# A hybrid mLSTM, HGRN2 and SwiGLU layer: operand sums of the gate input from the normalized rows in SBUF, in four two-row tiles, and a second norm emitted by readiness

## The chip, the cores and the metric

The kernel runs on one core of one Trainium2 chip. The metric is the device time of one launch in microseconds, as the median of several runs. A profiled execution has a time of its own; its trace names every instruction with its engine: TensorE (PE, with weight loads as PEld), VectorE (DVE), ScalarE (ACT), GpSimd (POOL) and SyncE (SP), whose queue issues nearly all DMAs.

## The reference

One layer for 1024 prompt tokens and 8 sequences of 4 new tokens (1056 columns in all), model width 1024. Cut to what matters:

```python
def _layer(x, ...):
    h = _rmsnorm(x, norm_mix)
    p = h @ w_in + b_in                       # split into mLSTM (q,k,v,o,i,f) and HGRN2 (q,f,i,g) parts
    out_a, ... = _mlstm_mixer(...)            # causal conv over 4 rows, chunked mLSTM, head norm, sigmoid gate
    out_b, ... = _hgrn_mixer(...)             # chunked HGRN2, head norm, silu gate
    x = x + concat([out_a, out_b]) @ w_out
    h2 = _rmsnorm(x, norm_ffn)                # the second norm
    x = x + (silu(h2 @ w_gate) * (h2 @ w_up)) @ w_down     # D_FF = 2816
    return x, states
y = _rmsnorm(x, norm_final)
```

The states of both mixers are returned too. All is float32.

## The kernel before, in words

Activations lie transposed: the 1024 features are 8 rows k (`KT`) of 128 partitions, the 1056 tokens are columns. Each float32 operand of a large product is split into a high and a low part of a reduced format (`HI`, `LO` for activations, `whi`, `wlo` for weights), and a product is three matmuls: HI by whi, LO by whi, HI by wlo. ACT copies the high part out, DVE or POOL subtracts to get the low part.

The stages, by the trace's time:

- 0 to 36 us: start, first norm of block 0. The tokens go in three blocks of 288, 384 and 384 (`BL`). Blocks 1 and 2 are normalized by the generator `startup(b)` while block 0's products run.
- to about 270 us: the w_in products of the mLSTM part, head by head and block by block, with the mixer's small products between them; `ck`, `qB` are a head's k and q after the convolution (L573 to L590 on DVE), `go` its output gate (L623 on ACT); L685 is the q-k product of a chunk.
- to about 550 us: the same for the HGRN2 part, and the sample sequences (`sample_b`), whose states come in by DMA (`st`, L774) for the products `so` (L842). The mixer's outputs are written into the rows of X; `mix_split` splits them into HI and LO, and `x_rows` reloads x into X for the residual.
- to about 649 us: the out-projection (w_out). `out_evac` adds the residual into X, squares the row (L1210) and adds the squares up (L1214) for the second norm, and stores X to DRAM (`d_x`), for the end of the kernel. The tokens go in four quarters q of 264 (`QN`) here. `norm2(q)` normalizes a quarter in place and splits it into HI and LO.
- to about 693 us: two "plain" feed-forward tiles (`NPLAIN`), 16 units of 24 matmuls; their evictions are a silu on ACT (L1250) and a product on DVE (L1256).
- to about 1200 us: gate and up products of the other 20 tiles in a seven-product scheme (`g_step`, P1 to P7, L1466), with operand sums T1 to T4 of the activations made by `t_prep` and `t3_prep`, and sums S1 to S4 of the weights made by `gsplit` (S on DVE L1383, whi on ACT L1394, wlo on POOL or DVE L1395). P1 and P2 take HI and LO as they are; P5 and P6 take T1 and T2. ACT copies P2's result out of PSUM (L1474).
- to the end: the down-projection (L1689) and the last norm.

X is one SBUF tile of 8 rows. `norm2` stores its normalized rows to a DRAM buffer `d_h` (L1224), and `t_prep` loads them back (`fetch`, L1310) into tiles in which it may overwrite them; X itself becomes the tile of T1 and T2.

The order of the work is written by the program itself. TensorE's units stand in a list; between its matmuls `hook()` lets generators such as `startup`, `norm2` and `t_prep` emit a step each. A generator that yields a number waits for so many hooks; one that yields `need(engine, tiles...)` waits until a running estimate of all engines' times (`estimate`) has those tiles ready. Each engine runs its instructions in the order emitted, so this fixes each queue.

```python
def x_rows(m, th):                 # called after the split of each odd row
def norm2(q):
    yield from norm_gen(("q", q), xq(q), hq(HI, q), hq(LO, q), naccs[q], V_G2, N2W[q], ...)
N2W = ((3, 3), (2, 4), (5, 4), (6, 4))     # counts of hooks before the norm's two TensorE steps
TPK0 = 6                           # plain unit before which t_prep starts
```

Of the kernel before, what the change touches and what calls it, by code (L numbers as in the profile page):

```python
# [41 lines left out]
def hybrid_step(ctx: ExitStack, tc: tile.TileContext, i, o):  # L42
# [197 lines left out]
    def emit_k(u, ks):  # L240
        t, nk = u["t"], u["nk"]
        rh, rl = u["rhs"]
        n = rh[:, 0, :].shape[1]
        if ks[0] == 0:
            u["ps"] = bank(u["tag"])
# [3 lines left out]
        for k in ks:  # L249
            c = k * u["stride"] + u["coff"]  # L250
            wh, wl = hi[:, c:c + 128], lo[:, c:c + 128]
            nc.tensor.matmul(ps[:, :n], wh, rh[:, k, :], start=(k == 0), stop=False)  # L252
            if not late:
                nc.tensor.matmul(ps[:, :n], wh, rl[:, k, :], start=False, stop=False)  # L254
            nc.tensor.matmul(ps[:, :n], wl, rh[:, k, :], start=False, stop=(k == nk - 1 and not late))  # L255
# [22 lines left out]
    X = act.tile([128, KT, T], F32, tag="X", name="X")  # L278
    x2 = [X]
# [19 lines left out]
    def load_x(b):  # L299
        for m in range(0, KT, 2):  # L300
            nc.sync.dma_start(xb(b)[:, m:m + 2], i["xT"][:, m:m + 2, OFF[b]:OFF[b] + BL[b]])
# [56 lines left out]
    def norm_gen(key, x, hv, lv, acc, vg, w=(2, 3), pb=None, lo_dve=(0, 4), step=2, rows=None, late=()):  # L358

        n = x.shape[2]  # L360
# [3 lines left out]
        def low(m):  # L364
            (nc.vector if m in lo_dve else nc.gpsimd).tensor_tensor(lv[:, m, :], x[:, m, :], hv[:, m, :].bitcast(F32),
                                                                    op=OP.subtract)
        for m in range(KT):
            nc.vector.scalar_tensor_tensor(x[:, m, :], x[:, m, :], col(vg + m), pb[:, :n], op0=OP.mult, op1=OP.mult)
            nc.scalar.activation(hv[:, m, :], x[:, m, :], AF.Copy)  # L369
            if m and m - 1 not in late:  # L370
                low(m - 1)
            if m == KT - 1:
                for j in (*late, m):
                    low(j)
            if rows and m % 2:
                rows(m - 1)
            if (m + 1) % step == 0:
                yield 1
# [39 lines left out]
    d_h = dram.tile([128, KT, T], F32, name="d_h")  # L418
# [243 lines left out]
    def mix_a(h, b):  # L662
# [93 lines left out]
        nc.vector.scalar_tensor_tensor(mo(b)[:, h, :], pH[:, :npr], col(V_MN + h), S["o", h, b][:, :npr],  # L756
# [172 lines left out]
    def mix_b(h, b):  # L929
# [196 lines left out]
        nc.vector.scalar_tensor_tensor(mo(b)[:, 4 + h, :], pH[:, :npr], col(V_HN + h), S["g", h, b][:, :npr],  # L1126
# [47 lines left out]
    def x_rows(m, th):  # L1174
        if th == 0:
            nc.sync.dma_start(X[:, m - 1:m + 1, 0:256], i["xT"][:, m - 1:m + 1, 0:256])
            nc.sync.dma_start(X[:, m - 1:m + 1, 256:528], i["xT"][:, m - 1:m + 1, 288:560])
        else:
            nc.sync.dma_start(X[:, m - 1:m + 1, 528:1024], i["xT"][:, m - 1:m + 1, 560:1056])

    def mix_split(th):
        hv, lv = half(HI, th), half(LO, th)
        n = 528 if th == 0 else 496
        if th:
            nc.sync.dma_start(X[:, :, 1024:1056], i["xT"][:, :, 256:288])
# [36 lines left out]
    def norm2(q):  # L1222
        def rows(m):
            nc.sync.dma_start(d_h[:, m:m + 2, q * QN:(q + 1) * QN], xq(q)[:, m:m + 2, :])  # L1224
# [69 lines left out]
    t3, t4t, TX = [], [None], []  # L1294

    def t_prep():
# [5 lines left out]
        ex = [sgtile(), sgtile()]  # L1302
        b = {}

        def fetch(m, th):

            if th == 0:
                t = ex if m in (5, 7) else rgtile()
                b[m] = t if m in (5, 7) else [t[:, 0:528], t[:, 528:1056]]
# [3 lines left out]
        for m in (0, 4, 1, 5):  # L1313
            while ("row", 3, m // 2 * 2) not in done:
                yield 1
            fetch(m, 1)
        TX.append(act.tile([128, KT * T], F32R, tag="X", name="T12"))
        T12 = TX[0]
        OPS["T1"], OPS["T2"] = [(q3(T12[:, quad(2 * j)]), q3(T12[:, quad(2 * j + 1)])) for j in range(2)]
        yield TPW[0]  # L1320
        for kk in range(4):
            b11, b12, b21, b22 = b[kk] + b[kk + 4]
            nc.vector.tensor_tensor(t3[kk], b22, b12, op=OP.subtract)
            done.add(("d3", kk))
            nc.vector.tensor_tensor(b12, b12, b11, op=OP.subtract)
            yield 1
            nc.vector.tensor_tensor(b22, b22, b12, op=OP.subtract)
            for n_, t, eng in (("T1", b12, nc.gpsimd), ("T2", b22, nc.gpsimd), ("T4", b21, nc.vector)):
                h, lw = OPS[n_][0][:, kk, :], OPS[n_][1][:, kk, :]
                if n_ == "T4":  # L1330
                    nc.vector.tensor_tensor(b21, b21, b22, op=OP.subtract)
                nc.scalar.activation(h, t, AF.Copy)
                if n_ == "T4":
                    yield 1
                eng.tensor_tensor(lw, t, h.bitcast(F32), op=OP.subtract)
# [3 lines left out]
            if kk == 2:
                gload(1)  # L1340
            if kk < 2:
                for m in (kk + 2, kk + 6):
                    fetch(m, 0)
                    fetch(m, 1)
            yield TPW[1]

    TPW = (3, 1)
    TPK0 = 6
# [102 lines left out]
    def g_step(u, p):  # L1451
        wn, bn = FACT[p]
        wh, wl = gw[u, wn]
        rh, rl = OPS[bn]
        for j in range(2):
# [7 lines left out]
            for kk in range(4):  # L1463
                w = slice(128 * kk, 128 * kk + 128)
                for x, (a, b_) in enumerate(((wh, rh), (wh, rl), (wl, rh))):
                    nc.tensor.matmul(ps[:, :QN], a[:, w], b_[:, kk, c], start=new and kk == 0 and x == 0,  # L1466
# [113 lines left out]
    def load_x2(m):  # L1580
        nc.sync.dma_start(x2[0][:, m:m + 2], d_x[:, m:m + 2])
# [87 lines left out]
    def d_step(g, p):  # L1669
# [5 lines left out]
        for j in range(2):  # L1675
# [16 lines left out]
            y = x2[0][:, 2 * mp_ + r, q * QN:q * QN + QN]  # L1692
# [30 lines left out]
    def plain(m, j):  # L1723
# [7 lines left out]
        y = x2[0][:, m, PN * j:PN * j + PN]  # L1731
# [171 lines left out]
    def startup(b):  # L1903
# [9 lines left out]
        for m in range(KT + 2):  # L1913
            if m < KT:
                yield need("DVE", pb, x[:, m, :])
                nc.vector.scalar_tensor_tensor(x[:, m, :], x[:, m, :], col(V_G1 + m), pb[:, :BL[b]], op0=OP.mult, op1=OP.mult)
            if 0 < m <= KT:
                nc.scalar.activation(hv[:, m - 1, :], x[:, m - 1, :], AF.Copy)
            if m > 1:
                e = nc.vector if now["DVE"] < now["POOL"] else nc.gpsimd  # L1920
                e.tensor_tensor(lv[:, m - 2, :], x[:, m - 2, :], hv[:, m - 2, :].bitcast(F32), op=OP.subtract)
            estimate()

    def startup0():
# [10 lines left out]
        for _ in norm_gen(0, xb(0), hb(HI, 0), hb(LO, 0), None, V_G1, pb=pb, lo_dve=(0, 3, 6), late=(0, 3, 6)):  # L1935
# [24 lines left out]
    for ui, u in enumerate(units + [None]):  # L1960
        if ui == units1:
            start(t3_prep(), ("t3",))
            gi, TPK = 2, 2
            for k, (gu_, p) in enumerate(steps):
# [20 lines left out]
                if (gu_, p) == (NU - 1, "P6"):  # L1985
                    x2[0] = act.tile([128, KT, T], F32, tag="X", name="X2")
# [203 lines left out]
```

## Time and profile before

| what | us |
|---|---|
| median of 3 runs | 1359.04 (1357.44 to 1359.11) |
| the profiled execution's own time | 1360.21 |
| its span | 1358.4 |
| TensorE busy in it | 1325.8 |
| VectorE, ScalarE, GpSimd busy | 860.1, 558.0, 594.1 |

The mean TensorE clock granted in the span was 0.986 of full speed. A profile row reads: start and duration in us, engine, line, operation, out<-in and its size, and in brackets the idle time of that engine just before and what ended it. In the list of waits a row is: engine and line that waited, what it waited for, total us, number of waits, longest.

### The profile page before, as it was taken

To read this page: it belongs to the slowest core of one execution; us is meant where nothing else is said; L and a number is where in the kernel's file an instruction comes from. 1 tells how busy PE (TensorE), PEld (TensorE's weight loads), DVE (VectorE), ACT (ScalarE), POOL (GpSimd) and SP (SyncE) were. 2 spreads that over 40 slices of the span, in tenths; PEclk is the share of its full clock that TensorE was granted. 3 is DMA by queue.
4 is the path that set the end of the run, shared out by engine and by line. 5 is a ranking of instruction groups with operands and counts; after the bars stand their busy time and mean duration, and the time that the engine had idled before them with its cause. 6 is when DMAs were issued, how large, how long until landed. Compare 5 with 4: busy or idle time off the path is not lost. (4 is left out here: it accounts for less than half of the span.)

```text
span 1358.4 us, 29355 instructions
## 1 busy us (share of the span) xinstructions
PE 1325.8 (98%) x11584; PEld 1295.0 (95%) x11584; DVE 860.1 (63%) x2051; ACT 558.0 (41%) x1309; POOL 594.1 (44%) x561
## 2 busy tenths in 40 slices
PE   7999999999999999999989999999999999999996
PEld 7999999899999998999989999999999999999995
DVE  7886666745555567536565676675664347777765
ACT  6663433244343445124345554455454332212232
POOL 4342322323121314025365656565666585444435
PEclk8999999999999999999989999999999999999997
DMA  9120212411010115633635675765764189878733
GB/s 357 27 95 30 87 51 80 136 46 48 19 48 19 50 41 177 196 110 130 222 123 198 218 241 212 249 217 204 251 212 158 60 297 351 294 280 295 270 146 128
DMA packets 111426, 216.44 MB, mean 159 GB/s; under 512 B 11265, under 2 KB 64409, under 8 KB 110777
## 3 DMA queue, kind: packets, MB, share of 16 engines
q1 hardware_dynamic: 110856, 214.31, 45.4%
q8 instruction: 91, 1.49, 0.4%
q14 instruction: 47, 0.38, 0.1%
q10 hardware_dynamic: 432, 0.27, 0.1%
HBM read 148.08 MB, written 66.45 MB: 158 GB/s over the span
## 5 line engine op out<-in xcount | busy, mean ns | idle before, releaser
L252 PE MATMUL mm<-HI,whi 128*128 128x384 f32 (+2 forms) x1160 | 378.3, 326 | 1.9 <-ACT HI L369 1.1
L255 PE MATMUL mm<-HI,wlo 128*128 128x384 f32 (+2 forms) x1160 | 361.9, 312 | 0.7 <-DVE wlo L213 0.7
L254 PE MATMUL mm<-LO,whi 128*128 128x384 f32 (+2 forms) x1136 | 352.2, 310 | 0.0
L252 PEld LDWEIGHTS mm<-HI,whi 128*128 128x128 f32 x1160 | 220.0, 190 | 7.0 <-issue 1.6
L255 PEld LDWEIGHTS mm<-HI,wlo 128*128 128x128 f32 x1160 | 220.0, 190 | 1.0 <-DVE wlo L213 0.9
L254 PEld LDWEIGHTS mm<-LO,whi 128*128 128x128 f32 x1136 | 214.4, 189 | 0.0
L213 POOL TENSOR_TENSOR wlo<-raw,whi 128x512 fp32r<-128x512 f32 x86 | 116.8, 1368 | 201.4 <-ACT whi L212 201.3
L1395 POOL TENSOR_TENSOR wlo<-S,whi 128x512 fp32r<-128x512 f32 x78 | 110.9, 1428 | 92.0 <-ACT whi L1394 90.2
L1466 PE MATMUL mx<-T,whi 128*128 128x264 f32 x640 | 118.5, 284 | 0.0
L1466 PEld LDWEIGHTS mx<-T,whi 128*128 128x128 f32 x640 | 99.3, 189 | 0.0
L1519 POOL TENSOR_TENSOR LO<-rg,HI 128x528 fp32r<-128x528 f32 x52 | 70.3, 1361 | 64.5 <-ACT HI L1518 64.4
L1466 PE MATMUL mx<-HI,whi 128*128 128x264 f32 x320 | 91.0, 284 | 0.0
L1466 PE MATMUL mx<-T,wlo 128*128 128x264 f32 x320 | 90.9, 284 | 0.0
L1466 PE MATMUL mx<-HI,wlo 128*128 128x264 f32 x320 | 90.9, 284 | 0.0
L1466 PE MATMUL mx<-LO,whi 128*128 128x264 f32 x320 | 90.7, 283 | 0.0
L1607 DVE TENSOR_TENSOR fh<-fr,fh 128x512 fp32r<-128x512 f32 x80 | 65.2, 815 | 30.5 <-ACT fh L1602 30.3
L1693 DVE TENSOR_TENSOR X<-X,mx 128x264 f32<-128x264 f32 x160 | 65.6, 424 | 26.1 <-PE mx L1689 25.6
L1394 ACT ACTIVATE whi<-S 128x512 fp32r<-128x512 f32 x80 | 50.3, 630 | 67.9 <-DVE S L1383 64.2
L1518 ACT ACTIVATE HI<-rg 128x528 fp32r<-128x528 f32 x52 | 32.3, 641 | 104.2 <-PE mx L1689 31.0
L1466 PE MATMUL mm<-HI,whi 128*128 128x264 f32 x240 | 68.3, 284 | 1.0 <-ACT nt L1250 1.0
L1466 PE MATMUL mm<-HI,wlo 128*128 128x264 f32 x240 | 68.2, 284 | 0.0
L1466 PE MATMUL mm<-LO,whi 128*128 128x264 f32 x240 | 67.9, 283 | 0.0
(548 smaller groups left out, 3412.1 us busy)
## 6 DMA issues: line engine op xcount, KB each, us to landing
d_wf<-fh SPq DMA_DIRECT2D x60, 512.0 KB, 3.0
rg<-d_ff SPq DMA_DIRECT2D x42, 528.0 KB, 9.4
raw<-in_wA SPq DMA_DIRECT2D x31, 512.0 KB, 3.6
whi<-d_wf SPq DMA_DIRECT2D x29, 512.0 KB, 4.5
wlo<-d_wf SPq DMA_DIRECT2D x28, 512.0 KB, 6.0
raw<-in_wgu SPq DMA_DIRECT2D x24, 512.0 KB, 4.4
d_ff<-sg SPq DMA_DIRECT2D x40, 264.0 KB, 2.6
rg<-in_wgu SPq DMA_DIRECT2D x20, 512.0 KB, 5.0
```

Of the source, the lines that this page charges most:

```text
L213: (nc.gpsimd if pool else nc.vector).tensor_tensor(lo[:, s], raw[:, s], hi[:, s].bitcast(F32), op=OP.subtract)
L252: nc.tensor.matmul(ps[:, :n], wh, rh[:, k, :], start=(k == 0), stop=False)
L254: nc.tensor.matmul(ps[:, :n], wh, rl[:, k, :], start=False, stop=False)
L255: nc.tensor.matmul(ps[:, :n], wl, rh[:, k, :], start=False, stop=(k == nk - 1 and not late))
L1394: nc.scalar.activation(hi[:, s], t, AF.Copy)
L1395: (nc.vector if dve else nc.gpsimd).tensor_tensor(lo[:, s], t, hi[:, s].bitcast(F32), op=OP.subtract)
L1466: nc.tensor.matmul(ps[:, :QN], a[:, w], b_[:, kk, c], start=new and kk == 0 and x == 0, stop=kk == 3 and x == 2, skip_group_check=True)
L1518: nc.scalar.activation(h, src, AF.Copy)
L1519: (nc.vector if dve else nc.gpsimd).tensor_tensor(lw, src, h.bitcast(F32), op=OP.subtract)
L1607: nc.vector.tensor_tensor(lw, src, h.bitcast(F32), op=OP.subtract)
L1693: nc.vector.tensor_tensor(y, y, ps[:, :QN], op=OP.add)
```

## The change

X becomes four tiles of two rows each, `X0` to `X3`, tile k holding rows k and k+4; products and norms take the rows in the order `PAIRS` (0, 4, 1, 5, 2, 6, 3, 7). `norm2` no longer stores to `d_h`; `t_prep` takes its sums straight from the tiles, with temporaries from the pools `fr` and `fh` that the down-projection uses later, and T1 and T2 become four tiles in the places of X0 to X3. `t_prep` may start at the fourth plain unit instead of the sixth. `norm2` is written out with `need` in place of counted hooks. The residual rows are reloaded in pairs after the split of row 4 and later, `d_x` is stored in pairs (16 stores instead of 8), and the last output store becomes two.

```diff
-    X = act.tile([128, KT, T], F32, tag="X", name="X")
+    Xt = [act.tile([128, 2, T], F32, tag=f"X{k}", name=f"X{k}") for k in range(4)]
+    PAIRS = [m for k in range(4) for m in (k, k + 4)]
+    def xr(m, c0=0, c1=T):
+        return Xt[m % 4][:, m // 4, c0:c1]
...
     def x_rows(m, th):
-        if th == 0:
-            nc.sync.dma_start(X[:, m - 1:m + 1, 0:256], i["xT"][:, m - 1:m + 1, 0:256])
-            nc.sync.dma_start(X[:, m - 1:m + 1, 256:528], i["xT"][:, m - 1:m + 1, 288:560])
-        else:
-            nc.sync.dma_start(X[:, m - 1:m + 1, 528:1024], i["xT"][:, m - 1:m + 1, 560:1056])
+        for d0, d1, s0 in ((0, 256, 0), (256, 528, 288)) if th == 0 else ((528, 1024, 560), (1024, 1056, 256)):
+            nc.sync.dma_start(Xt[m - 4][:, :, d0:d1], xT2[:, :, m - 4, s0:s0 + d1 - d0])
...
-            if m % 2:
+            if m > 3:
                 x_rows(m, th)
...
-            if m in (4, KT - 1):
-                s = slice(0, 5) if m == 4 else slice(5, KT)
-                nc.sync.dma_start(d_x[:, s, q * QN:(q + 1) * QN], x[:, s, :])
+            if m > 3:
+                c = slice(q * QN, (q + 1) * QN)
+                nc.sync.dma_start(d_x.rearrange("p (two k) t -> p two k t", two=2)[:, :, m - 4, c], Xt[m - 4][:, :, c])
...
     def norm2(q):
-        def rows(m):
-            nc.sync.dma_start(d_h[:, m:m + 2, q * QN:(q + 1) * QN], xq(q)[:, m:m + 2, :])
-            done.add(("row", q, m))
-        yield from norm_gen(("q", q), xq(q), hq(HI, q), hq(LO, q), naccs[q], V_G2, N2W[q], lo_dve=(0, 2, 4, 6), rows=rows)
-    N2W = ((3, 3), (2, 4), (5, 4), (6, 4))
+        ...
+        yield need("PE", acc, banks=1, lead=-0.4)
+        pc = bank()
+        for t, c in parts:
+            nc.tensor.matmul(pc[:c, t:t + 1], acc[:, 128 * t:128 * t + c], ones, start=True, stop=True)
+        yield need("DVE", pc)
+        ...
+        yield need("PE", rs, banks=1, lead=-0.4)
+        ...
+        for j in range(KT + 2):
+            if j < KT:
+                m = PAIRS[j]
+                yield need("DVE", pb)
+                nc.vector.scalar_tensor_tensor(x(m), x(m), col(V_G2 + m), pb[:, :n], op0=OP.mult, op1=OP.mult)
+                if j % 2:
+                    done.add(("row", q, j // 2))
+            ...
     def t_prep():
...
-            nc.sync.dma_start(b[m][th], d_h[:, m, 528 * th:528 * th + 528])
-        for m in (0, 4, 1, 5):
-            fetch(m, 0)
...
+        gload(1)
...
+            for q in range(4):
+                while ("row", q, kk) not in done:
+                    yield need("DVE")
+            xs_ = (xr(kk), xr(kk + 4))
+            (b11, b12), (b21, b22) = [(x[:, 0:528], x[:, 528:T]) for x in xs_]
+            yield need("DVE", *xs_)
+            nc.vector.tensor_tensor(t3[kk], b22, b12, op=OP.subtract)
+            f1 = temp("fr")
+            nc.vector.tensor_tensor(f1, b12, b11, op=OP.subtract)
+            ...
+            f2 = temp("fh")
+            nc.vector.tensor_tensor(f2, b22, f1, op=OP.subtract)
+            nc.vector.tensor_tensor(b21, b21, f2, op=OP.subtract)
+            ...
+            nc.scalar.activation(h4, b21, AF.Copy)
+            nc.vector.tensor_tensor(l4, b21, h4.bitcast(F32), op=OP.subtract)
+            y = act.tile([128, 2, T], F32R, tag=f"X{kk}", name=f"T{kk}")
+            for j, f in enumerate((f1, f2)):
+                h, lw = y[:, j, 0:528], y[:, j, 528:T]
+                nc.scalar.activation(h, f, AF.Copy)
+                nc.gpsimd.tensor_tensor(lw, f, h.bitcast(F32), op=OP.subtract)
...
-    TPK0 = 6
+    TPK0 = 4
...
-        nc.sync.dma_start(o["yT"][:, m:m + n, c], x2[0][:, m:m + n, c])
+        for r in range(m, m + n, 2):
+            nc.sync.dma_start(o["yT"][:, r:r + 2, c], x2t[r // 2][:, :, c])
```

Because the estimate sees other tiles and other times, the emitted order moves at more places than the diff names. Three of them follow. Line numbers after the change run 10 to 30 higher.

ACT's queue at the norm of block 1 (34 to 40 us before), first as it was, where `v` and `go` are evictions of head 0's first products, L1890 is a square for block 1 or 2 and L1918 the high parts of block 1's rows:

```order
L625 ACTIVATE v<-mx,vec 128x288
L1918 ACTIVATE HI<-X 128x384 x3
L1890 ACTIVATE raw,nrs<-raw 128x1024
L623 ACTIVATE go<-mx,hbo 128x288
L1918 ACTIVATE HI<-X 128x384 x5
```

and as it is now (L598 is the tanh of the convolution's q, L588 before):

```order
L635 ACTIVATE v<-mx,vec 128x288
L598 ACTIVATE raw<-qB 128x288
L633 ACTIVATE go<-mx,hbo 128x288
L1913 ACTIVATE raw,nrs<-raw 128x1024
L1943 ACTIVATE HI<-X_78 128x384 x2
L1943 ACTIVATE HI<-X_79 128x384 x2
```

The tanh, the gate and the square now stand ahead of all of block 1's copies, where three copies stood ahead of them. On DVE the convolution rows of k (`ck`) likewise stand ahead of block 1's rows now.

ACT's queue at the end of the plain units (about 690 to 704 us before). T_8360 and T_8342 are T1/T2 and T4, and the last row is the copy of P2's result:

```order
L1394 ACTIVATE whi<-S 128x512
L1332 ACTIVATE T_8360<-sg 128x528
L1332 ACTIVATE T_8342<-sg 128x528
L1394 ACTIVATE whi<-S 128x512
L1250 ACTIVATE nt<-mm 128x264
L1357 ACTIVATE HI<-sg 128x528
L1394 ACTIVATE whi<-rg 128x512
L1394 ACTIVATE whi<-S 128x512
L1357 ACTIVATE HI<-sg 128x528
L1394 ACTIVATE whi<-rg 128x512
L1394 ACTIVATE whi<-raw 128x512
L1474 ACTIVATE nt<-mm 128x264
```

and now, where T_8280 is T4 and T_8554 the last of T1/T2's tiles:

```order
L1356 ACTIVATE T_8280<-X_81 128x528
L1364 ACTIVATE T_8554<-fr 128x528
L1364 ACTIVATE T_8554<-fh 128x528
L1416 ACTIVATE whi<-raw 128x512
L1281 ACTIVATE nt<-mm 128x264
L1416 ACTIVATE whi<-S 128x512 x2
L1281 ACTIVATE nt<-mm 128x264
L1379 ACTIVATE HI<-sg 128x528
L1416 ACTIVATE whi<-rg 128x512
L1416 ACTIVATE whi<-S 128x512
```

The last of the T copies stands two evictions (L1281) ahead of the copies for T3 (`HI<-sg`) instead of one; the rows from there to P2's copy are the same.

SP's queue around the sample states (about 500 to 516 us before):

```order
L774 DMA st<-in_S 128x4x128 x3
L1176 DMA X<-in_xT 128x2x256
L1177 DMA X<-in_xT 128x2x272
L774 DMA st<-in_S 128x4x128 x2
L1176 DMA X<-in_xT 128x2x256
```

and now:

```order
L784 DMA st<-in_S 128x4x128 x6
L1186 DMA X_78<-in_xT 128x2x256
L1186 DMA X_78<-in_xT 128x2x272
L784 DMA st<-in_S 128x4x128
L1186 DMA X_79<-in_xT 128x2x256
```

Six state fetches now stand ahead of the first residual reload instead of three.

More of the change, by code (lines that the diff above doesn't have):

```diff
@@ L243, in emit_k @@
         n = rh[:, 0, :].shape[1]
+        kp = PAIRS if nk == KT else range(nk)
         if ks[0] == 0:
@@ L299, in load_x @@
     def load_x(b):
-        for m in range(0, KT, 2):
-            nc.sync.dma_start(xb(b)[:, m:m + 2], i["xT"][:, m:m + 2, OFF[b]:OFF[b] + BL[b]])
+        for k in range(4):
+            nc.sync.dma_start(Xt[k][:, :, OFF[b]:OFF[b] + BL[b]], xT2[:, :, k, OFF[b]:OFF[b] + BL[b]])
     xn = {}
@@ L356, in norm_rstd, with norm_gen, low @@
         return pb
-    def norm_gen(key, x, hv, lv, acc, vg, w=(2, 3), pb=None, lo_dve=(0, 4), step=2, rows=None, late=()):
-        n = x.shape[2]
+    def norm_gen(key, n, x, hv, lv, acc, vg, w=(2, 3), pb=None, lo_dve=(0, 4), step=2, rows=None, late=()):
         if pb is None:
             pb = yield from norm_rstd(key, n, acc, w)
[L364 to L377, printed above, removed]
+        def low(j):
+            m = PAIRS[j]
+            (nc.vector if j in lo_dve else nc.gpsimd).tensor_tensor(lv[:, m, :], x(m), hv[:, m, :].bitcast(F32), op=OP.subtract)
+        for j, m in enumerate(PAIRS):
+            nc.vector.scalar_tensor_tensor(x(m), x(m), col(vg + m), pb[:, :n], op0=OP.mult, op1=OP.mult)
+            nc.scalar.activation(hv[:, m, :], x(m), AF.Copy)
+            if j and j - 1 not in late:
+                low(j - 1)
+            if j == KT - 1:
+                for y in (*late, j):
+                    low(y)
+            if rows and j % 2:
+                rows(j // 2)
+            if (j + 1) % step == 0:
                 yield 1
@@ L1339, in t_prep @@
[L1339 to L1347, printed above, removed]
-    TPK0 = 6
+            f1 = temp("fr")
+            nc.vector.tensor_tensor(f1, b12, b11, op=OP.subtract)
+            yield need("DVE", f1)
+            f2 = temp("fh")
+            nc.vector.tensor_tensor(f2, b22, f1, op=OP.subtract)
+            yield need("DVE", f2)
@@ L1349, in hybrid_step @@
+        for j in range(2):
+            OPS[f"T{1 + j}"] = [[hl[k, j][x] for k in range(4)] for x in range(2)]
+        done.add(("t12",))
+    TPK0 = 4
     GSK = 11
@@ L1453, in g_step @@
         wh, wl = gw[u, wn]
-        rh, rl = OPS[bn]
+        rh, rl = [x if isinstance(x, list) else [x[:, k, :] for k in range(4)] for x in OPS[bn]]
         for j in range(2):
@@ L1465, in g_step @@
                 for x, (a, b_) in enumerate(((wh, rh), (wh, rl), (wl, rh))):
-                    nc.tensor.matmul(ps[:, :QN], a[:, w], b_[:, kk, c], start=new and kk == 0 and x == 0,
+                    nc.tensor.matmul(ps[:, :QN], a[:, w], b_[kk][:, c], start=new and kk == 0 and x == 0,
                                      stop=kk == 3 and x == 2, skip_group_check=True)
@@ L1912, in startup @@
         x, hv, lv = xb(b), hb(HI, b), hb(LO, b)
[L1913 to L1919, printed above, removed]
+        for j in range(KT + 2):
+            if j < KT:
+                m = PAIRS[j]
+                yield need("DVE", pb, x(m))
+                nc.vector.scalar_tensor_tensor(x(m), x(m), col(V_G1 + m), pb[:, :BL[b]], op0=OP.mult, op1=OP.mult)
+            if 0 < j <= KT:
+                m = PAIRS[j - 1]
+                nc.scalar.activation(hv[:, m, :], x(m), AF.Copy)
+            if j > 1:
+                m = PAIRS[j - 2]
                 e = nc.vector if now["DVE"] < now["POOL"] else nc.gpsimd
[L1921 removed]
+                e.tensor_tensor(lv[:, m, :], x(m), hv[:, m, :].bitcast(F32), op=OP.subtract)
             estimate()
@@ L1985, in hybrid_step @@
                 if (gu_, p) == (NU - 1, "P6"):
-                    x2[0] = act.tile([128, KT, T], F32, tag="X", name="X2")
+                    x2t.extend(act.tile([128, 2, T], F32, tag=f"X{k}", name=f"X2{k}") for k in range(4))
                     load_x2(0)
```

112 lines of the change are left out of this document (56 added, 56 removed).

## The prediction

> **What bounds the kernel now.** I read the page first, then TensorE's list of waits, then windows around each wait for the clock, then the timeline of the engine that each wait names.
>
> ```profile
> PE 1325.8 (98%) x11584; PEld 1295.0 (95%) x11584; DVE 860.1 (63%) x2051; ACT 558.0 (41%) x1309; POOL 594.1 (44%) x561
> ...
> PEclk8999999999999999999989999999999999999997
> ...
> PE 46%; DVE 1%; issue 0%; ACT 0%; POOL 0%; POOLq 0%; ACTq 0%
> ```
>
> TensorE is busy for 98% of a span of 1358.4 us, and the chain that ended last names almost nothing else. The diff neither adds nor drops a matmul (10,280 TensorE instructions in both built programs), so only two things can move the time: microseconds in which TensorE stands idle, and stretches in which its clock is granted at half.
>
> ```profile
> PE mm L1466 <- ACT nt L1474: 3.2, 1, 3.2
> ...
> PE mx L685 <- DVE ck L590: 2.0, 1, 2.0
> PE so L842 <- DMA st<-in_S: 1.7, 1, 1.7
> ...
> PE mx L347 <- DVE W L1214: 1.2, 1, 1.2
> ...
> PE mm L1466 <- ACT nt L1250: 1.0, 1, 1.0
> ...
> PE mm L252 <- ACT HI L1918: 0.4, 2, 0.2
> ```
>
> These are the waits within the change's reach; each row is the total, the number of waits and the longest. By window (length, then busy time of PE, PEld, DVE, ACT, POOL, then the clock, the DMA share and GB/s):
>
> ```profile
> 199.00:205.00 6.00, 4.55 (x23) 4.55 (x24) 3.02 (x8) 3.05 (x6) 3.19 (x3) 0.72 0.26 90
> 512.00:519.00 7.00, 5.26 (x35) 4.16 (x34) 5.60 (x12) 2.11 (x5) 4.01 (x6) 0.76 0.74 221
> 638.00:648.00 10.00, 8.49 (x68) 8.06 (x67) 5.53 (x14) 5.78 (x12) 7.72 (x7) 1.00 0.39 136
> 693.00:700.00 7.00, 5.95 (x49) 5.74 (x48) 5.49 (x8) 3.22 (x7) 2.77 (x3) 1.00 0.06 19
> 700.00:710.00 10.00, 6.76 (x34) 6.54 (x33) 6.05 (x6) 5.99 (x14) 10.00 (x8) 0.66 0.14 37
> 710.00:720.00 10.00, 10.00 (x84) 10.00 (x84) 2.54 (x6) 4.63 (x10) 6.40 (x5) 1.00 0.72 258
> ```
>
> The wait of 3.2 us lies in 700 to 710, where the clock was 0.66. That window ran 34 matmuls; the next, same shapes and full clock, ran 84, so one matmul is 10/84 = 0.119 us and the window lost 50 of them, 5.95 us. The window from 693 lost 58.8 - 49 = 9.8 of them, 1.17 us. Together 7.1 us: the largest hole after startup. Waits of 1.97 us (199 to 205) and 1.74 us (512 to 519) went with a low clock too: 6 x 0.28 = 1.68 us and 7 x 0.24 = 1.68 us of lost clock. The waits of 1.16 and 1.05 us (638 to 648, 693 to 700) did not.
>
> [...]
>
> **A. The end of the plain feed-forward units (620 to 710 us).**
>
> ```profile
> L1224 SPq DMA_DIRECT2D d_h<-X x16: 359/360/480, 626.2 to 659.9; - x16
> ...
> 670.11 0.71 DVE L1323 TENSOR_TENSOR sg<-rg 128x528 f32<-128x528 f32 x1 [5.28 <-DMA rg<-d_h]
> ...
> 696.61 0.71 DVE L1335 TENSOR_TENSOR T<-sg,T 128x528 fp32r<-128x528 f32 x1 [0.71 <-ACT T L1332]
> ...
> 699.56 1.78 DVE L1383 TENSOR_TENSOR S<-raw 128x512 f32<-128x512 f32 x1
> ...
> 698.49 0.37 ACT L1250 ACTIVATE nt<-mm 128x264 f32<-128x264 f32 x1
> ...
> 701.38 0.63 ACT L1394 ACTIVATE whi<-S 128x512 fp32r<-128x512 f32 x1 [1.46 <-DVE S L1383]
> ...
> 703.48 0.37 ACT L1474 ACTIVATE nt<-mm 128x264 f32<-128x264 f32 x1
> ...
> 703.90 0.81 PE L1466 MATMUL mm<-T,whi 128*128 128x264 f32 x2 [3.24 <-ACT nt L1474]
> ```
>
> In order: the last normalized row goes to DRAM at 659.9; DVE idles 5.28 us until a reload lands, starts the operand sums at 670.11 and ends them at 697.3; the weight sum S comes behind them on DVE; ACT waits for it (1.46 us) with the copy of P2 queued behind; and P5's matmul waits for that copy, 3.24 us, after 1.05 us for a silu eviction of the same backlog.
>
> The change takes the 16 stores and 16 reloads out and lets DVE start when the fourth quarter's rows are normalized. They were at 659.9, when their stores went out. So the sums can start between 5.3 us (the DMA wait alone) and about 9 us (670.1 - 661) sooner. The order bears this out in kind: T-prep stands some 60 large matmuls earlier, 60 x 0.119 = 7 us. At the same pace of 27.2 us the sums end at 688 to 692 instead of 697.3. Everything behind them on DVE and ACT moves by as much, and 5.3 us is more than the 3.24 + 1.05 = 4.3 us of lateness. What is next there is the same list of ACT copies (the second place shown above, in the section on the change): with DVE off the path they end some 2 us before the copy is wanted, at 703.90 - 3.24 = 700.66. I take the whole 7.1 us; if a wait near 1 us remains, 6. The lower end is 0 (DVE is not sooner), the upper 7.1.
>
> A price against it: T-prep's temporaries add no operation (DVE's, ACT's and POOL's counts agree), but DVE's sums now run while POOL still subtracts for norm2.
>
> ```profile
> L1383 DVE TENSOR_TENSOR S<-raw x20: 677/684/1799, 691.7 to 1069.0; 128x512 f32<-128x512 f32 x20
> ```
>
> One and the same DVE sum takes 0.68 us in the median and 1.80 at most. T-prep's 16 sums stretched by 1.1 us each would be 18 us, more than the 5 to 9 gained; but the 27.2 us were measured with POOL at its own eight subtractions already, so I add nothing and leave it to the rivals.
>
> [...]
>
> **B. Evictions of the out-projection.** The 1.16 us wait (L347 on W) is a square sum queued on DVE behind norm rows that were emitted by a count of hooks. In the new order norm rows come when they are estimated ready and TensorE's sums for them stand later. Gain 0 to 1.2, I take 1.0. The DRAM stores of x, 16 instead of 8, hang on no engine but SP: 0.36 us of issue each like d_h's stores, with no TensorE wait named for them.
>
> **C. HGRN sample states (505 to 530 us).**
>
> ```profile
> 509.54 0.92 SPq L774 DMA_DIRECT2D st<-in_S  x2
> ...
> 514.84 0.42 PE L842 MATMUL so<-st,qz 128*32 128x128 f32 x8 [1.74 <-DMA st<-in_S]
> ```
>
> The state that TensorE waits for was fetched behind residual reloads on SP. With pairs (k, k+4) no reload is issued before the split of row 4, so six state fetches stand ahead of the first reload (third place shown), but the matmuls that use them stand 6 to 9 large matmuls sooner (about 1 to 1.5 us) and the seventh and eighth fetch have reloads ahead. Bounds: 1.74 + 1.68 = 3.4 gained, 2 lost. I take 0.
>
> **D. The mLSTM chunk at 200 us.**
>
> ```profile
> 195.36 3.83 DVE L583 SCALAR_TENSOR_TENSOR ck<-raw,vec,ck 128x384 f32<-128x384 f32 x3 [0.33 <-ACT ck L561]
> ...
> 200.45 0.94 PE L685 MATMUL mx<-qB,ck 128*128 128x128 f32 x6 [1.97 <-DVE ck L590]
> ```
>
> TensorE waits here for DVE's convolution. In the new order six more large matmuls stand ahead of this product, each about 0.17 us in this stage: the wait shrinks by 1.0 us to about 0.9, of the size that did not halve the clock. Gain 1.0 + 1.7 = 2.7 if so, 1.0 if the clock halves anyway, 0 if DVE is later too. I take 2.0.
>
> **E. The first norm of block 1 (34 to 46 us), the loss.**
>
> ```profile
> 34.15 2.17 DVE L1916 SCALAR_TENSOR_TENSOR X<-X,vec,mx 128x384 f32<-128x384 f32 x4
> ...
> 43.66 0.16 DVE L573 COPY raw<-hist 128x3 f32<-128x3 f32 x1
> ...
> 45.62 0.24 DVE L586 SCALAR_TENSOR_TENSOR ck<-rs,vec,ck 128x32 f32<-128x32 f32 x1
> ...
> 34.78 1.57 ACT L1918 ACTIVATE HI<-X 128x384 fp32r<-128x384 f32 x3 [1.69 <-DVE X L1916]
> ...
> 36.26 1.04 ACT L1890 ACTIVATE raw<-raw 128x1024 f32<-128x1024 f32 x1
> ...
> 37.30 0.48 ACT L623 ACTIVATE go<-mx,hbo 128x288 f32<-128x288 f32 x1
> ...
> 39.35 1.05 ACT L1918 ACTIVATE HI<-X 128x384 fp32r<-128x384 f32 x2 [0.32 <-DVE X L1916]
> ...
> 36.05 0.44 PE L255 MATMUL mx<-HI,wlo 128*128 128x288 f32 x1
> ...
> 42.32 0.33 PE L252 MATMUL mm<-HI,whi 128*128 128x384 f32 x1
> ```
>
> Block 1's rows now stand behind DVE's ten convolution rows for k (43.66 to 45.86, 2.2 us), and ACT's HI copies behind `go` and the 1.04 us square. DVE alone would start rows at 34.15 + 2.2 = 36.35. ACT decides: `go` reads the product whose last matmul ends near 36.5, so `go` runs to 37.0, the square with its read-out to 38.2, the first copy to 38.7, where TensorE wants it at about 36.3: a wait of 2.4 us. Eight copies at 0.45 to 0.52 us end near 41.9 instead of 40.4, and the unit that ended at 42.32 ends 1.5 us later, 1.9 with a transpose that stands three matmuls sooner. A 2.4 us wait is of the size that halved the clock elsewhere; then up to 1.7 us more. Loss 1.9 to 3.6 by these rows; 1 to 5 with the unknown. I take 3.0.
>
> **F. The rest.** Mix steps move by up to 69 large matmuls either way, and a final store becomes two issues (0.4 us on SP, beside other stores). No row prices this; the nearest are the waits of 0.3 to 2 us listed. I take -0.3 and bounds of 2 either way.
>
> **Sum.** Gains 7.1 + 1.0 + 0 + 2.0, losses 3.0 + 0.3: 6.8 us. The profiled execution took 1360.21 us; 1353.4. The median of the runs is 1.17 us below it (1359.04 against 1360.21), so 1352.3 for the median; I state 1352.7, a little back for a small remnant of the wait in A. 0.2% of this kernel is 2.7 us, about what a measurement can tell from no change.
>
> **The rivals.**
> 1. *The hole at 700 us stays.* DVE's sums start sooner but stretch among norm rows and POOL's subtractions, or the backlog on ACT was the silu and weight copies' own. For it: DVE sums of 1.5 to 1.8 us. Against it: DVE stood idle 5.28 us for the reload. Then A is 0: 1359.0 + 7.1 - 6.8, about 1359.5. Chance 0.12.
> 2. *Slower: T-prep blocks the evictions.* DVE is in order; its sums now stand between the up-projection's evictions (L1256), and the three mm banks are TensorE's only cover, two units of 24 x 0.119 = 2.9 us each. If T-prep's 27.2 us grows past 36 with the norm rows mixed in, it ends after 701, TensorE waits 4 us more than before and the clock loss stays: 1359.5 + 4, about 1363. It decides from an end of the sums 3 us later than now. Chance 0.08.
> 3. *The early loss is double.* Two half-clock stretches and a mix step that waits at 45 to 70 us: 7 us in place of 3, 1356.7; with A at 6, 1358. Chance 0.16.
> 4. *No early loss, and C gains.* 1352.7 - 3, less C's part: 1348.5. Chance 0.14.
>
> **How the numbers follow.** The forecast, A to F as summed, has 0.50, with its own range 1350 to 1356. Faster by over 0.2% (under 1356.3): 0.50 + 0.14 + about 0.08 of rival 3 = 0.72. The same: 0.08 of rival 3 and 0.10 of rival 1 = 0.18. Slower (over 1361.8): 0.02 of rival 1 and rival 2 = 0.10. The range from 1347.5 (rival 4 with the whole of C) to 1359 (rival 3, and the near edge of rival 1) leaves out about 2 in 10.
>
> **What would show it.** A: no wait of L1466's successor on the P2 copy, clock 1.00 from 700 to 710, first operand sum at 665 or earlier in the same count. B: no wait for W before the norm's sums. D: clock near 1.00 around the chunk. E: a wait of about 2 us for the HI copy at 36 us and a block-1 unit that ends near 44 to 46. C: the wait on st gone or of the same size. Wrong would be: the operand sums begin no sooner, or a new wait over 3 us in the mix phases.

## The result, and the profile after

The changed kernel takes 1364.57 us in the median of six runs (1362.57 to 1365.96), the kernel before 1358.76 in six runs beside it: a ratio of 1.0044, 95% interval 1.0031 to 1.0057. It is 5.8 us slower; 1352.7 was forecast. The profiled execution took 1364.32 us with a span of 1362.3. From the page after the change:

```profile
PE 1326.3 (97%) x11584; PEld 1293.9 (95%) x11584; DVE 875.2 (64%) x2051; ACT 555.3 (41%) x1309; POOL 593.3 (44%) x561
...
PEclk8999999999999999999999999999999999999997
```

TensorE's own work is what it was (1326.3 us busy against 1325.8), and the span is 3.9 us longer. Among TensorE's waits after the change are these:

```profile
PE mx L743 <- DVE C L730: 2.5, 1, 2.5
PE mx L702 <- DVE kt L712: 2.1, 1, 2.1
PE so L852 <- DMA st<-in_S: 2.1, 2, 1.3
PE mm L254 <- ACT HI L1943: 2.0, 1, 2.0
PE mm L257 <- DVE wlo L213: 1.9, 2, 1.0
...
PE mx L695 <- DVE ck L600: 0.3, 1, 0.3
```

The two waits at 700 us (3.2 and 1.0) and the 2.0 at 200 us (now 0.3) are gone. In their place stand a wait for the state update C, one for kt and one for block 1's high parts, all before 240 us. By window (columns as in the prediction):

```profile
36.00:46.00 10.00, 7.87 (x33) 6.25 (x32) 8.28 (x15) 7.09 (x16) 4.93 (x5) 0.79 0.29 80
95.00:106.00 11.00, 8.46 (x47) 8.02 (x46) 10.59 (x22) 6.03 (x18) 5.36 (x4) 0.69 0.37 129
208.00:214.00 6.00, 5.72 (x38) 5.40 (x37) 5.21 (x8) 2.16 (x5) 3.90 (x3) 1.00 0.74 238
232.00:240.00 8.00, 5.85 (x38) 5.64 (x37) 5.66 (x22) 3.14 (x8) 3.03 (x8) 1.00 0.00 0
...
702.00:712.00 10.00, 9.98 (x82) 9.72 (x81) 5.45 (x9) 6.23 (x14) 7.53 (x6) 1.00 0.09 30
```

702 to 712 runs 82 matmuls at full clock where the same stage ran 34 in 10 us. The loss is at 36 to 46 (clock 0.79) and above all at 95 to 106, where TensorE stands 2.5 us and the clock is 0.69: 11 x 0.31 = 3.4 us more.

Both programs issue the large matmuls in the same sequence of units, so the start of the nth large matmul (a matmul of split operands) can be compared in the two traces. Late is positive; each row is the growth of that difference over a stretch.

| stretch of before, us | start of its last large matmul: before, after (us) | forecast | measured |
|---|---|---|---|
| to 20 | 20.5, 21.9 | 0 | +1.3 late |
| 20 to 60 (E) | 60.2, 65.9 | +3.0 | +4.4 |
| 60 to 106 (F) | 106.3, 118.5 | +0.3 with the rest of F | +6.5 |
| 106 to 198 (F) | 198.1, 210.7 | | +0.3 |
| 198 to 211 (D) | 211.3, 220.6 | -2.0 | -3.2 |
| 211 to 301 (F) | 301.2, 312.7 | | +2.2 |
| 301 to 637 (C) | 636.8, 647.7 | 0 | -0.7 |
| 637 to 666 (B) | 665.6, 675.3 | -1.0 | -1.2 |
| 666 to 709 (A) | 709.3, 712.2 | -7.1 | -6.8 |
| to the end | 1335.8, 1339.6 | 0 | +0.9 |

The sum is +3.7 us, close to the 3.9 by which the spans of these two executions differ; the medians lie further apart since the profiled execution of before was one of its slower ones. A and B came as forecast, D gained a little more. F cost 9.0 us where 0.3 was taken.

Where F went, in the timeline after the change from 88 to 98 us (DVE, then POOL and PE):

```profile
89.03 0.55 DVE L715 SCALAR_TENSOR_TENSOR W<-mx,W 128x384 f32<-128x384 f32 x1
89.61 0.55 DVE L462 SCALAR_TENSOR_TENSOR gB<-gA,gB 4x384 f32<-4x384 f32 x1
...
90.25 4.04 DVE L467 TENSOR_TENSOR_SCAN gC<-ones,gB 4x128 f32<-4x128 f32 x3
94.22 0.98 DVE L469 TENSOR_TENSOR_SCAN gm<-gB,mcar,gA 4x384 f32<-4x384 f32 x1
...
97.62 1.12 DVE L730 SCALAR_TENSOR_TENSOR C<-C,wib,mx 128x129 f32<-128x129 f32 x3
...
90.03 3.99 POOL L213 TENSOR_TENSOR wlo<-raw,whi 128x512 fp32r<-128x512 f32 x3 [3.08 <-ACT whi L212]
...
98.03 0.55 PE L743 MATMUL mx<-C,qw 128*128 128x129 f32 x2 [2.54 <-DVE C L730]
```

DVE makes kt and W of one chunk, then 8.0 us of gate scans for block 2 (L462 to L479), and only then the state update C for which TensorE waits. DVE runs its queue in order: the product that C reads (L720) had ended at 92.4, but C starts at 97.62. The two half-clock stretches of the window lie right behind this wait: from 98.3 to 105.1 us the granted clock was 0.50.

### The profile page after: what moved, and what is told of

Same layout as the page of the kernel before. It is cut to its first block, busy times and chain, and to the rows that moved or that the text cites. A ratio compares the mean times of both kernels' runs of the same rounds, so it can differ in the third digit from the quotient of the medians.

```text
span 1362.3 us, 29321 instructions
## 1 busy us (share of the span) xinstructions
PE 1326.3 (97%) x11584; PEld 1293.9 (95%) x11584; DVE 875.2 (64%) x2051; ACT 555.3 (41%) x1309; POOL 593.3 (44%) x561
## 4 chain that ended last, share of the span: by engine, by line
PE 87%; DVE 8%; ACT 2%; issue 2%; POOL 1%; DMA 1%; POOLq 0%; DVEq 0%; ACTq 0%
PE mx L1488 17%; PE mm L254 11%; PE mm L257 10%; PE mm L256 10%; PE mm L1488 10%; PE mx L1711 8%; PE mm L1711 5%; PE so L1488 3%; PE mx L971 1%; PE mx L823 1%; PE so L1711 1%; PE mx L1752 1%; PE mm L1752 1%; DVE ck L593 1%; PE mx L1093 1%
## 5 line engine op out<-in xcount | busy, mean ns | idle before, releaser
L257 PEld LDWEIGHTS mm<-HI,wlo 128*128 128x128 f32 x1160 | 220.6, 190 | 3.4 <-DVE wlo L213 2.4
L213 POOL TENSOR_TENSOR wlo<-raw,whi 128x512 fp32r<-128x512 f32 x86 | 114.4, 1339 | 202.6 <-ACT whi L212 202.5
```

What stands on the lines that cost most here:

```text
L213: (nc.gpsimd if pool else nc.vector).tensor_tensor(lo[:, s], raw[:, s], hi[:, s].bitcast(F32), op=OP.subtract)
L257: nc.tensor.matmul(ps[:, :n], wl, rh[:, kk, :], start=False, stop=(k == nk - 1 and not late))
```

## The experiments

Each ratio is to runs of the kernel before on the same chip.

### Which part of the change loses

Rows 0 to 7 again in the w_in products and the norms ahead of them; the rest as changed:

```diff
-        kp = PAIRS if nk == KT else range(nk)
+        kp = PAIRS if nk == KT and t >= wo[0] else range(nk)
...
-        for j, m in enumerate(PAIRS):          # norm_gen, block 0; and the same in startup(b)
+        for j, m in enumerate(range(KT)):
```

> The kernel after, but the w_in products (and the norms that feed them) take the rows in the order 0 to 7 again; tiles, sums from SBUF and the second norm as changed. All queues up to the out-projection are then those of before. Theory Q (the loss of some 11 us before 290 us comes from the row order in pairs, by way of the queues that the estimate writes): the early loss is gone, the gains at 645 and 700 us stay, 1358.8 - 1.2 - 7 = 1350.5 us, ratio about 0.994. Rival T (the loss comes from the four tiles and their loads): 1362 to 1365.

Measured: 1351.47 us, ratio 0.9942 (0.9928 to 0.9956). This version beats both kernels, the changed one by 13 us. The loss comes with the row order of the first stage.

The other half, in the kernel before: only that row order, with its loads in pairs.

```diff
+    PAIRS = [m for k in range(4) for m in (k, k + 4)]
...
+        kp = PAIRS if nk == KT and t < wo[0] else range(nk)
...
+            kk = kp[k]
...
-            nc.tensor.matmul(ps[:, :n], wh, rh[:, k, :], start=(k == 0), stop=False)
+            nc.tensor.matmul(ps[:, :n], wh, rh[:, kk, :], start=(k == 0), stop=False)
```

> The kernel before with one part of the change: the w_in products and their norms take the rows in pairs (0, 4, 1, 5, ...); X one tile, DRAM buffer and second norm as before. The queues up to the out-projection become those of after. Theory Q: all of the early loss and nothing of the gain, 1358.8 + 9 to 11, about 1369. Rival T: near 1359.

Measured: 1371.24 us, ratio 1.0084 (1.0069 to 1.0100): all of the loss, with the hole at 700 still there. Its list of waits has both:

```profile
PE mm L1471 <- ACT nt L1479: 3.3, 1, 3.3
...
PE mx L738 <- DVE C L725: 2.5, 1, 2.5
PE mm L254 <- ACT HI L1925: 2.2, 2, 2.0
```

0.9942 x 1.0084 is 1.0025; the ends of the two intervals multiply to 0.9996 and 1.0056, and the 1.0044 of the whole change lies between. No third part is needed.

### Is it the rows or the queues

Two kernels separate them. What is emitted at each hook up to the out-projection comes from a table, written by the other row order:

```diff
     def hook(part=False):
         estimate()
+        if fixed:
+            for k in fixed.pop(0):
+                step_gen(next(e for e in active if e[1] == k))
+            return
```

> As e2, but what is emitted at each hook up to the out-projection is taken from a table written by the kernel before, so that every engine's queue stands as before and only the row numbers differ. Theory Q: 1 to 2 us slower than before (the second row of a product now needs the second half of its weight tile, which hurts at the start only), about 1360.5. Rival W (the pairs themselves cost, since each product waits for both halves of its split weight): 1366 to 1369.

Measured: 1358.69 us, ratio 0.9995 (0.9986 to 1.0005). The pair order in the old queues costs nothing that can be measured, less than the 1 to 2 us expected. At 20 us it is 2.0 us late (TensorE waits twice for the second half of wlo, 0.7 and 1.0), but a later wait of 1.67 us is gone for it, and at 60 us it is 0.2 us ahead.

> The kernel before, rows 0 to 7, with what is emitted at each hook up to the out-projection taken from a table written by e2. Theory Q: the waits at 40, 98 and 237 us appear, 1366 to 1368. Rival W: about 1359 to 1360.

Measured: 1372.90 us, ratio 1.0104 (1.0081 to 1.0127), more than expected. Rows 0 to 7 in the new queues have the waits of the change:

```profile
PE mx L784 <- DVE C L771: 3.6, 1, 3.6
...
PE mm L303 <- ACT HI L1969: 2.4, 2, 2.0
```

So the queues lose, and the row order only by way of them. How it gets there can be read in the code: `estimate` keeps a ready time for each 512-column half of a split weight, and in pairs a product's second row is row 4, which reads the second half. The estimate then sets TensorE's time in the first products differently, `need` compares with that time, and steps fall on other hooks. With one ready time for a whole weight, both row orders of the kernel before give the same queues, instruction for instruction; such a kernel was not run.

### Which entries of the queues lose

In the changed kernel, one entry of its own table moved: block 2's scans, from behind kt and W to ahead of them.

```diff
 hook 148: (a,0,2) x4
+          (g,2)
 ...
-hook 154: (a,0,1) x4, (g,2), ...
+hook 154: (a,0,1) x4, ...
```

> The kernel after, with its own steps up to the out-projection from a table in which one entry is moved: VectorE's gate scans of block 2 (L462 to L479 of after, 8.0 us from 89.6) are emitted six hooks earlier, ahead of the chunk's kt product instead of between it and the state update C. Theory Q1 (the C update behind the scans costs the 2.54 us wait at 98 us, and that wait the two half-clock stretches from 98.3 to 105.1, 3.4 us): both go, 1364.6 - 5.9 = 1358.7. Rival (the wait only moves to kt or to the gates' transposes, or the clock halves there anyway): 1362 or more.

Measured: 1358.94 us, ratio 0.9994 (0.9984 to 1.0004), as expected. TensorE no longer waits for C, and the clock is whole:

```profile
90.00:106.00 16.00, 14.03 (x109) 13.42 (x110) 12.26 (x31) 8.60 (x25) 9.41 (x8) 1.00 0.55 175
```

One step of one generator was worth 5.6 us by the medians and 6.8 by the ratios, 3.4 of it clock. In the trace the stretch from 60 to 106 us now loses 2.5 us instead of 6.5: a wait of 1.24 us for kt has come up at 105 us. The edit changed two things at once, since the moved scans no longer ran beside POOL's subtractions (POOL stands idle there until 84.99) and were shorter, 1.03 us where they took 4.04:

```profile
80.82 1.03 DVE L518 TENSOR_TENSOR_SCAN gC<-ones,gB 4x128 f32<-4x128 f32 x3
```

Then block 1's rows ahead of the convolution of k:

```diff
-hook 41: ..., (cv,k,0,0), ...        hooks 49 to 56: (n1,1) one row each
+hooks 43, 45, 46, 49 to 52: (n1,1), two rows at 43; (cv,k,0,0) at hook 57
```

> The kernel after, with its own steps from a table in which block 1's norm rows stand ahead of VectorE's convolution of k, one or two rows a hook, as in before. Theory Q2 (block 1's rows behind the convolution, and ScalarE's copies behind the tanh, the gate and the square, cost the 2.04 us wait at 39.6 and a half-clock stretch of 1.7): 1364.6 - 3.5 = 1361. Rival (the start loses because the second row of a product needs the second half of its weight, which stays here): 1364 to 1365.

Measured: 1363.01 us, ratio 1.0028 (1.0018 to 1.0038), against 1.0044 (1.0031 to 1.0057) for the whole change: about 2 us better, less than the 3.5 expected, and the intervals overlap.

```profile
PE mx L545 <- ACT gB L533: 1.5, 1, 1.5
...
PE mm L305 <- ACT HI L1994: 1.2, 2, 1.0
```

The wait of 2.0 us became 1.0 and the mean clock of the span was 0.990 where it was 0.987, but a new wait of 1.5 us came up at 73 us, for block 1's gates from ScalarE. In the trace the stretch from 20 to 60 us loses 1.1 us instead of 4.4, as Q2 has it, and the one from 60 to 106 loses 8.6 instead of 6.5, which takes 2 us of the gain back.

### What closed the hole at 700 us

The trip put back into e1, store and reload in place:

```diff
+                dk = d_h.rearrange("p (two k) t -> p two k t", two=2)[:, :, k, 528:T]
+                nc.sync.dma_start(dk, Xt[k][:, :, 528:T])
+                nc.sync.dma_start(Xt[k][:, :, 528:T], dk)
```

> e1 with a round trip through DRAM put back: before its sums each pair of normalized rows, columns 528 to 1055, is stored to DRAM and loaded back into the same tile. Theory D (the trip is what made the sums late): the first sum about 5 us later, part of the waits at 699 and 704 us back, 1354 to 1358. Rival N (the sums were late for where the steps were emitted, and the trip's 5 us are spare): 1351.5, no wait.

Measured: 1389.06 us, ratio 1.0217 (1.0200 to 1.0234), far outside what either theory gave. This is no test of the old trip. SP's queue is in order too: each reload waits in it for its own store to land, 5.4 to 7.8 us from one issue to the other, with the next pair behind it, and the reload into the same tile makes later readers wait:

```profile
L1346 SPq DMA_DIRECT2D d_h<-X x4: 524/568/612, 660.9 to 681.8; - x4
L1347 SPq DMA_DIRECT2D X<-d_h x4: 567/567/572, 667.5 to 689.5; - x4
...
  POOL LO L1258: 25.7, 1
```

So the two candidates, trip and emission, were crossed instead. First the start:

```diff
-    TPK0 = 4
+    TPK0 = 6
```

> e1 with the operand sums allowed from the sixth plain unit again instead of the fourth. Two units are 5.7 us. Theory D: the rows of the fourth quarter are ready only about then, so at most 2 to 3 us of spare time go: 1351.5. Rival N: the earlier start was the gain: 1354 to 1358.

Measured: 1352.43 us, ratio 0.9945 (0.9932 to 0.9957), the same as e1 (0.9942): the earlier permission is worth nothing that can be measured. Then the readiness without the SBUF path, in the kernel before:

```diff
     def norm2(q):                       # body as in after, rows 0 to 7
+                if j % 2:
+                    nc.sync.dma_start(d_h[:, j - 1:j + 1, q * QN:(q + 1) * QN], x[:, j - 1:j + 1, :])
```

> The kernel before with one part of the change: the second norm emitted by readiness, as in after, its rows stored to DRAM and reloaded as before. TensorE's queue from the out-projection on is then that of after. Theory D (the trip through DRAM makes the operand sums late): the 1.16 us wait at 645 us goes, the waits of 1.05 and 3.24 us at 700 stay, 1359.5 - 1.2 = 1358.3. Rival N (the emission made them late): the hole at 700 closes too, 1352.

Measured: 1360.59 us, ratio 1.0007 (0.9994 to 1.0020), a little over the 1358.3 expected. The trace gains 1.2 us between 637 and 666 us and loses 1.5 between there and 709: the hole stays, even wider, in its waits

```profile
PE mm L1493 <- ACT nt L1501: 3.3, 1, 3.3
...
PE mm L1493 <- ACT nt L1277: 2.2, 1, 2.2
```

and in the window, with 35 matmuls:

```profile
700.00:710.00 10.00, 6.04 (x35) 5.83 (x36) 5.69 (x7) 7.25 (x16) 8.75 (x7) 0.83 0.05 15
```

And the SBUF path without the readiness, in e1:

```diff
-    def norm2(q): ...                   # need
+        yield from norm_gen(("q", q), QN, xq(q), ..., N2W[q], ..., od=PAIRS)
+    N2W = ((3, 3), (2, 4), (5, 4), (6, 4))
```

> e1 with the second norm emitted by counts of hooks as in before; sums from SBUF, no trip. Theory D: the hole at 700 stays closed, the 1.16 us wait at 645 is back, 1351.5 + 1.2 = 1352.7. Rival N: the hole is back, 1357 or more.

Measured: 1355.48 us, ratio 0.9972 (0.9959 to 0.9984). The hole is closed; the wait at 645 us is back and in this execution took a half-clock stretch with it:

```profile
700.00:710.00 10.00, 10.00 (x84) 10.00 (x83) 5.06 (x5) 5.36 (x13) 10.00 (x8) 1.00 0.45 158
644.00:652.00 8.00, 7.04 (x46) 6.79 (x46) 2.98 (x9) 2.97 (x6) 2.79 (x3) 0.79 0.21 73
```

With the trip the hole is there whether the norm is emitted by counts (before) or by readiness (e9); without it the hole is closed both ways (e10 and e1). So the path through SBUF closed it, and not the norm's emission. In e9 DVE itself stands idle for the reload, ahead of the first sum; in e10 the first sum starts 7.6 us earlier:

```profile
671.94 0.71 DVE L1350 TENSOR_TENSOR sg<-rg 128x528 f32<-128x528 f32 x1 [7.68 <-DMA rg<-d_h]
...
664.30 0.71 DVE L1318 TENSOR_TENSOR sg<-X 128x528 f32<-128x528 f32 x1 [1.88 <-DMA d_ff<-go]
```

The path is more than the trip left out: the four tiles, the temporaries and T-prep's own places in the queues came with it, and no run separates these.

Readiness is the gain at 645 us. By the medians e10 lies 4.0 us above e1, more than the 1.2 expected; in the two traces 2.7 us of that stand between 637 and 666 us, about 1.7 of it clock (8 x 0.21). A wait for the sample states, 2.3 us in e10 against 1.9 in e1, lies outside what was edited.

### Moving one product

In e1 with its own table, the q-k product at 200 us and all later steps of that chunk four hooks later:

```diff
-hooks 356 to 374: the second step of 356 and all later ones of (a,2,2)
+the same, each 4 hooks later
```

> e1 with its own steps from a table in which the q-k product of head 2, block 2 (200 us) and what follows it in that chunk are emitted four hooks, 12 large matmuls, 2.1 us later. If that wait is only a matter of place: the 1.95 us are gained, and 1.7 more in runs in which the clock halved there, 1348 to 1349.5. Rival (the chunk's next steps wait instead): 1351.5.

Measured: 1355.23 us, ratio 0.9966 (0.9952 to 0.9979): no gain. The rival holds; the next product of the chunk waits as long as the first did:

```profile
205.22 0.57 PE L774 MATMUL mx<-vt,kt 128*128 128x129 f32 x3 [1.94 <-DVE kt L766]
```

In the changed kernel the product is also later by six matmuls, but there the whole stage's queues are others. That 12 matmuls more do not help in e1 shows that D's gain is no matter of this product's place alone. Why e11 ends some 3.8 us above e1 is not settled. In the two traces it is 1.9 us: 1.1 between 211 and 301 us, behind the moved steps, and 0.9 between 520 and 560, with larger waits at 523 and 546 us, where nothing was edited.

## Why the prediction was right or wrong

**A was right in its mechanism, and its size fitted.** Forecast 7.1, measured 6.8. The sums began at once when the rows were normalized, and before, e1, e9 and e10 together show that the path through DRAM, not the norm's emission, made them late:

```profile
671.35 0.48 DVE L1249 SCALAR_TENSOR_TENSOR X<-X,vec,mx 128x264 f32<-128x264 f32 x1
...
672.09 0.69 DVE L1345 TENSOR_TENSOR sg<-X 128x528 f32<-128x528 f32 x1
...
695.43 0.71 DVE L1358 TENSOR_TENSOR T<-X,T 128x528 fp32r<-128x528 f32 x1
...
708.49 0.37 ACT L1496 ACTIVATE nt<-mm 128x264 f32<-128x264 f32 x1
```

At this point the trace is 9.7 us late, so the first sum stands 7.7 us sooner than before (672.09 - 9.7 = 662.4 against 670.11), within the 5.3 to 9 worked out; they take 24.1 us, not 27.2, so as a whole the sums did not stretch. The copy of P2 comes 4.7 us sooner in the same count. The size owes something to luck: 3.4 of the 7.1 us were clock (10 x 0.34), and a hole with a wait of 3.3 us went with a clock of 0.83 in e9 and of 1.00 in e3.

**B was right** in the trace (1.2 against 1.0); e10 shows that with the clock it can be worth more. **C** was taken at 0 and gave 0.7; the state's wait is there in every kernel, 1.5 to 3.0 us in all. **D** gave 3.2 where 2.0 were taken, and its parts can be read from the trace:

```profile
211.73 0.56 DVE L600 SCALAR_TENSOR_TENSOR ck<-raw,ck 128x384 f32<-128x384 f32 x1 [0.65 <-ACT raw L598]
...
212.35 0.94 PE L695 MATMUL mx<-qB,ck 128*128 128x128 f32 x6 [0.28 <-DVE ck L600]
```

The trace is 12.5 us late here, so the convolution ends 0.6 us sooner than before (212.29 - 12.5 = 199.8 against 200.40), which was not foreseen; the six matmuls make 1.0, as forecast; and the half-clock stretch of 1.7 us is not there (1.00 from 208 to 214 us). That last part is not the change's alone: in e1, with the old place and a wait of 1.95 us, the clock stayed whole as well (1.00 from 195 to 207 us).

**E had the mechanism right and the size too small.** The trace is 1.3 us late when TensorE begins to wait. Less this, the gate ends at 36.8 (37.0 was worked out), the square with its read-out at 37.9 (38.2), and TensorE goes on at 38.3 (38.7) after a wait of 2.04 us (2.4). A low clock followed, 0.55 from 40 to 43 us.

```profile
37.61 0.50 ACT L633 ACTIVATE go<-mx,hbo 128x288 f32<-128x288 f32 x1 [2.87 <-PE mx L257]
38.01 1.05 ACT L1913 ACTIVATE raw<-raw 128x1024 f32<-128x1024 f32 x1
38.96 0.19 ACT L1913 ACTIVATION_READ_ACCUMULATOR raw<-raw 128x1 f32 x1
39.05 1.76 ACT L1943 ACTIVATE HI<-X 128x384 fp32r<-128x384 f32 x4
...
39.62 0.46 PE L254 MATMUL mm<-HI,whi 128*128 128x384 f32 x1 [2.04 <-ACT HI L1943]
```

The stretch lost 4.4 us, within 1 to 5 but not the 3.0 of the sum, and the 1.3 us before 20 us were not seen at all: the second row's need for the second half of wlo (waits of 0.9 and 1.0 on L213).

**F is the step that failed.** "Mix steps move by up to 69 large matmuls either way", "No row prices this", "I take -0.3 and bounds of 2 either way": it cost 9.0 us, 6.5 at 60 to 106, 0.3 to 198 and 2.2 at 211 to 301. For want of a row, it put at next to nothing what a new neighbour in DVE's queue can cost. In the new order the gate scans of block 2 stand between a chunk's W and its C, and e5 shows that this is the loss there: 2.5 us of idleness and 3.4 of clock.

Half of a price stood in the trace of before. There the same scans, of block 1, stand in such a place, from 60.14 to 65.12, and nothing waits:

```profile
60.78 1.03 DVE L457 TENSOR_TENSOR_SCAN gC<-ones,gB 4x128 f32<-4x128 f32 x3
```

At this length, 3.0 us less than the 4.04, the C that TensorE had at 98.03 would have been there at about 95.0, and TensorE asked for it at 95.5 (98.03 - 2.54): by this estimate the order alone would not have cost a wait. The order and the stretch together did, and e5 took both away at once. That DVE's rows stretch could be seen as well: the 0.68 to 1.80 us of S were weighed in A, and not here. The bound of 2 us came from waits in the old queues, while what changes is which waits there are.

The other 2.2 us are of the same kind at 237 us: kt stands behind eight small rows of constants on DVE, the last of them 1.29 us long, and TensorE waits 2.15 us for it. No run moved these rows, so this is read from the trace and not shown.

```profile
234.84 1.29 DVE L420 TENSOR_SCALAR omlb<-lb 128x4 f32<-128x4 f32 x1
236.16 0.42 DVE L712 TENSOR_TENSOR kt<-mx,cols 128x256 f32<-128x256 f32 x1
...
236.72 0.41 PE L702 MATMUL mx<-ident,cq 128*128 128x128 f32 x2 [2.15 <-DVE kt L712]
```

Of the rivals the third, the early loss, at 0.16, named the right place; its size (7 in place of 3) fell short, since the stretches to 106 us cost 12.2. The second's time, about 1363, lies nearest to the measured one, but by its number only: it has the operand sums end later, and they ended 11 us sooner (695.43 + 0.71 - 9.7 = 686.4 against 697.3). One sum of the prediction does not come out: rival 4 with the whole of C is 1352.7 - 3.0 - 3.4 = 1346.3, not the 1347.5 given as the low end.

## What to carry to other kernels

When a program's emission order comes from a running estimate, an edit of the first stage's access order can be an edit of every queue: look at each engine's new order for long work that now stands between a producer and the product waiting for it, and price each such place with its idle time, with the lengths its rows took in the traces (here 1.03 or 4.04 us for the same three scans), and with the clock stretch that may follow (here none, or 1.7 to 3.4 us of lost clock). Then cross the parts: here one part of the change gained 8 us and another lost more, and they separate in two lines. Keeping the emission in a table while the rows change tells the order's cost from the data's.

## What the runs showed of the hardware that was not expected

The same wait of 2.0 us at 200 us (1.97 in before, 1.95 in e1) went with a clock of 0.86 from 195 to 207 us in the executions of before and e9, and of 1.00 in those of e1 and e10, in kernels whose queues agree there. First the window of e1:

```profile
195.00:207.00 12.00, 10.05 (x67) 9.60 (x67) 8.79 (x18) 5.64 (x11) 6.10 (x5) 1.00 0.36 124
```

and of e9, with the same busy time at a clock of 0.86:

```profile
195.00:207.00 12.00, 10.03 (x55) 9.71 (x54) 8.11 (x17) 4.71 (x10) 6.09 (x5) 0.86 0.33 116
```

The waits at 700 us did the same: in e3 they are 1.4 and 3.3 us, no shorter than before, and the clock stays whole where it was 0.66.

```profile
700.00:710.00 10.00, 6.66 (x53) 6.24 (x52) 6.05 (x7) 7.06 (x16) 10.00 (x7) 1.00 0.11 32
```

Even a wait of 1.1 us (e10 at 645) went with a low clock, 0.79 from 644 to 652 us, where 1.16 and 1.05 us in the kernel before had gone with 1.00. So in these executions the length of a wait did not settle whether a half-clock stretch came with it, and from them a forecast can give such a stretch a chance and no more.

DVE's short scan took 0.39 us in the kernel before from 60 to 81 us, and up to 1.44 where three of POOL's subtractions (90.03 to 94.02) ran beside it. The line's instructions before (least, median and most ns):

```profile
L457 DVE TENSOR_TENSOR_SCAN gC<-ones,gB x6: 386/388/402, 60.8 to 80.9; 4x128 f32<-4x128 f32 x6
```

and after:

```profile
L467 DVE TENSOR_TENSOR_SCAN gC<-ones,gB x6: 386/862/1436, 64.6 to 92.9; 4x128 f32<-4x128 f32 x6
```

The three before C took 4.04 us where three of the others take 1.03: 3.0 of the 8.0 us in front of C. In e5, with POOL idle, the same three take 1.03 again. That POOL is the reason is argued from these rows; no run moved POOL's work alone.
